# Steps listed from a block's landing, and a third column group turned by TensorE

## The chip, the cores and the metric

The kernel runs on one core of one Trainium2 chip. The metric is device time in microseconds (us) of one execution of the whole kernel; lower is better.

## What is computed

One layer of a streaming encoder on 512 frames of width 2048, in float32. One input projection feeds three token mixers of four heads each (forgetting, chunked and stick-breaking attention), a SiLU gate for each mixer and three merge gates for each channel. Then each mixer's output is projected up, weighted by its merge gate, the three are added, and one output projection is added to the input. The change lies in these last lines of the reference:

```python
    gates = jax.nn.sigmoid(proj[..., QKVG_COLS + N_HEADS:] + b_gate).reshape(b, s, N_BRANCH, D_MODEL)
    ...
    ys = ys * jax.nn.silu(br[:, :, :, 3])
    up = jnp.einsum('bsnw,nwd->bsnd', ys, w_up)
    merged = jnp.sum(gates * up, axis=2)
    return x + jnp.einsum('bsd,de->bse', merged, w_out)
```

## The kernel before

**Numbers.** A float32 product is made of three products of rounded parts: an operand is split into a high part (an ACT copy that rounds) and a low part (a DVE subtraction). For weights these are the tiles `wh` (L409) and `wl` (L419), for the other operand a `Parts` tile of both; `split` (L255 to L264) makes the latter. All main matmuls are L277. The input and output projections are done by Strassen's scheme with seven products, so they need differences of quarters of their operands too.

**Stages.** First the input projection with the attention of the heads beside it. Then the up projection, on which this case turns: its result `merged` is 512 frames by 2048 channels, in four *column groups* g of 512 channels. For each group and each of the three mixers (`UPS`, L1554, gives the order) there are two units of 24 matmuls (`up_units`, L1310). A unit treats its four row blocks of 128 frames one after another, six matmuls each. When a row block's sum stands in an accumulator (there are six, `accs`), `taken` (L1317) multiplies it by the gate, which ACT has put through a sigmoid (`gates_of`, L1297, line L1305) after a read from DRAM (L293): L1321, and for the second and third mixer adds it up: L1328. The order of `UPS` is groups 0 and 2 mixed, then group 1, then group 3. So group 1 is the third one done.

**Turning a group.** The output projection needs `merged` with channels on the partitions, so each group of 512 by 512 must be transposed. There are two ways. For groups in `DRAMS` (L1555: 0, 2 and 1), `folded` (L1350) lets DVE transpose 32x32 squares (L1354) and stores the four row blocks to DRAM (L301), and `turned_m` (L1361) reads each of the group's four channel blocks back with `back` (L307, four reads of 64 KB, L312), so that the squares land in their places. For the rest (group 3), `spun_m` (L1378) lets TensorE transpose (L1385) into a PSUM tile of which there are two (`atts`), four 128x128 transposes for each channel block, and ACT copies it out (L1392).

**Steps on a merged block.** `arrived` (L1370) numbers the blocks k = 4g + i and starts the steps that make the operands of the output projection's Strassen scheme. Blocks 0 to 7 (groups 0 and 1) get `merged_a` (L1398): one DVE subtraction (L1401) and a split (L258 on ACT, L262 on DVE) give `m1`. Blocks 8 to 15 (groups 2 and 3) get `merged_b` (L1406): they wait for `m1` of block k - 8, then make three differences (L268) and split them into `m23`, `m4` and `m2`. The first four units of the output projection use `m1` of blocks 0 to 3, the next four that of blocks 4 to 7 (`out_task`, L1461).

**What sets the order.** Each engine executes its own list of instructions in order, and the lists are written by a planner (`Flow`, L65) in the kernel's own program. A task is a generator that yields an engine and a cost for each step. The planner keeps a clock for each engine, takes the step that can start first and breaks ties by the due time, which is the time at which the task was ready plus its slack (L126). So a task's ready time and slack decide where a step stands in its engine's list. Nothing is decided again on the chip: there a step whose data isn't there yet holds all that stands behind it in the list. Transfers have a model of their landing (`landing`, L283, with `LAND` 3.5 and for `back` `PIECES` 4.0, L1560), in plan time. `spawn(gen, slack, ready)` starts a task; `flow.fin` is the planned end of the step that was just listed, and `flow.ready` the ready time of the task that is being advanced, which includes an event that it has passed. In `turned_m`, the last event before `arrived` is the landing plus `MEXTRA` (L1367). An event whose time is known doesn't stop a task, so `arrived` runs as soon as the last read is listed, and `flow.fin` is then the planned end of that read's issue (0.54 us for a read).

**Slots.** The tiles of 128x512 float32 (`t2s`, `NT` = 20 of them) serve gates, sums, merged blocks, differences and more. A task waits in the plan until one is free, and one with a slack over 1 leaves three (`KEPT`) free. `folded` gives the four tiles of a group back at the planned landing of their stores, `spun_m` gives all four back when the last of the group's channel blocks has been transposed, and takes a tile for each block at the copy.

**Other lists.** All reads and stores named here stand in SP's list with the loads of weights; POOL issues accumulating loads (L320) alone.

Of the kernel before, what the change touches and what calls it, by code (L numbers as in the profile page):

```python
# [25 lines left out]
UK = 8  # L26
# [38 lines left out]
class Flow:  # L65
# [16 lines left out]
    def give(self, slots, n=1):  # L82
        slots.free += [self.fin] * n

    def spawn(self, gen, slack, ready=None):
        task = Task(gen, slack, self.now if ready is None else ready)
        self.tasks.append(task)
        self.advance(task)
# [82 lines left out]
def dve_us(n, x=1):  # L171
    return x * (0.1 + 0.00105 * n)
# [3 lines left out]
def hybrid_kernel(  # L176
# [30 lines left out]
    flow = Flow()  # L207
    spawn, set_, give = flow.spawn, flow.set, flow.give
# [3 lines left out]
    def t2(s, dt=F32):  # L212
        return tp.tile([P, S], dt, tag="t2", name=nm(s))
# [13 lines left out]
    def blk(i):  # L227
        return slice(i * P, (i + 1) * P)
# [3 lines left out]
    def two(ap):  # L232

        return ap.rearrange("p (h s) -> p h s", h=2)
# [20 lines left out]
    def split(hi, lo, src, n, ev=None, due=(), hi_ev=None):  # L255

        yield (ACT, act_us(n), *due)
        nc.scalar.activation(hi, src, AF.Copy)  # L258
        if hi_ev is not None:
            set_(hi_ev)  # L260
        yield (DVE, dve_us(n), *due)
        nc.vector.tensor_sub(lo, src, f(hi))  # L262
        if ev is not None:
            set_(ev)  # L264

    def minus(to, a, b):

        nc.vector.scalar_tensor_tensor(to, a, -1.0, b, op0=ALU.mult, op1=ALU.subtract)  # L268
# [38 lines left out]
    def back(to, src):  # L307

        n = src.shape[0] * 4
        for b in range(4):  # L310
            yield issue(0.54)
            nc.sync.dma_start(to[32 * b:32 * (b + 1), :].rearrange("p (n c) -> p n c", c=32),  # L312
                              src.rearrange("t (a r) c -> (t a) r c", r=32)[:, :, 32 * b:32 * (b + 1)]
                              .rearrange("n r c -> r n c"))
            ev = Event(landing(flow.fin, n * 4, 128) + PIECES)
        return ev
# [60 lines left out]
    def at(u, g, slack=5.0):  # L377
        side.setdefault(u, []).append((g, slack))
# [971 lines left out]
    def folded(g, tb):  # L1350
        yield merged_ev[NB - 1, g, tb]
        m = merged[g, tb]
        yield DVE, dve_us(S) + 0.07
        nc.vector.transpose(m, m)  # L1354
        if g not in md:
            md[g] = dp.tile([QB, P, S], F32, name=nm("md"))
        md_ev[g, tb].t = (yield from store(md[g][tb], m, 256, t2s)).t + LATER
# [3 lines left out]
    def turned_m(g, i):  # L1361
        for tb in range(QB):
            yield md_ev[g, tb]
        yield t2s, 1
        m = t2("m")
        ev = yield from back(m, md[g][:, :, blk(i)])
        yield Event(ev.t + MEXTRA)  # L1367
        arrived(g, i, m)

    def arrived(g, i, m):  # L1370
        k = 4 * g + i
        if k < UK:
            kept_m[k] = m
            spawn(merged_a(k, m), 4.0, flow.fin)
        else:
            spawn(merged_b(k - UK, m), 3.0, flow.fin)

    def spun_m(g, i):  # L1378
        for tb in range(QB):
            yield merged_ev[NB - 1, g, tb]  # L1380
        yield atts, 1
        yield PE, 0.11 * QB
        ps = att()
        for tb in range(QB):
            nc.tensor.transpose(ps[:, blk(tb)], merged[g, tb][:, blk(i)], identf)  # L1385
        turns[g] = turns.get(g, 0) + 1
        if turns[g] == QB:
            give(t2s, QB)
        yield t2s, 1
        yield ACT, act_us(S)  # L1390
        m = t2("m")
        nc.scalar.activation(m, ps, AF.Copy)  # L1392
        give(atts)
        arrived(g, i, m)
# [3 lines left out]
    def merged_a(k, a):  # L1398

        yield DVE, dve_us(HS)  # L1400
        nc.vector.tensor_sub(a[:, RH], a[:, LH], a[:, RH])  # L1401
        yield xps, 1
        m1[k] = Parts("m1", [m1_ev[k]] * 2)
        yield from split(m1[k].hi, m1[k].lo, two(a), S, m1_ev[k])

    def merged_b(k, b):  # L1406
        a = kept_m[k]
        yield m1_ev[k]
        yield t2s, 1
        t = t2("mt")  # L1410
        if k % 2 == 0:
            yield t2s, 1
            mus[k // 2] = t2("mu")
        u = mus[k // 2][:, RH if k % 2 else LH]
        q = DVE, dve_us(HS)
        yield q
        minus(t[:, LH], b[:, RH], a[:, RH])
        yield q
        minus(t[:, RH], t[:, LH], a[:, LH])
        give(t2s)  # L1420
        yield q
        minus(u, t[:, LH], b[:, LH])
        yield xps, 1
        ev = Event()
        m23[k] = Parts("m23", [ev, ev])
        yield from split(m23[k].hi, m23[k].lo, two(t), S, ev)
        give(t2s)
        if k % 2 == 0:
            yield xps, 1
            m4[k // 2] = Parts("m4")  # L1430
            set_(m4_ev[k // 2])
        yield xps, 1
        ev = Event()
        m2[k] = Parts("m2", [ev, ev])
        yield from split(m2[k].hi, m2[k].lo, two(b), S, ev)
        give(t2s)
        yield m4_ev[k // 2]
        h, lo, ev = m4[k // 2].half(k % 2)
        yield from split(h, lo, u, HS, ev)
        if k % 2:  # L1440
            give(t2s)

    for g, b in UPS:
# [5 lines left out]
        for i in range(QB):  # L1449
            if g in DRAMS:  # L1450
                at(len(units) - 1, lambda g=g, i=i: folded(g, i))
# [100 lines left out]
NR = 8  # L1552

UPS = [(0, 0), (0, 1), (2, 0), (2, 1), (0, 2), (2, 2)] + [(g, b) for g in (1, 3) for b in range(3)]  # L1554
DRAMS = (0, 2, 1)  # L1555
MLATE, MSKIP = 2.5, 1

EARLY = 0.5
# [4 lines left out]
HSLACK = 12.0  # L1563
ENDSLACK, ENDOFF = 3.0, 3
EARLYG = 1
MEXTRA = 8.0

_OUT = (QB, NQ, P, S)

# [45 lines left out]
```

## Time and profile before

| | us |
|---|---|
| median of 3 runs | 1297.6 |
| lowest and highest run | 1290.79, 1299.38 |
| the profiled execution, its own time | 1294.25 |
| span of the profiled execution | 1292.5 |
| TensorE busy | 1274.2 (99%) |
| VectorE (DVE) busy | 999.5 (77%) |
| ScalarE (ACT) busy | 752.2 (58%) |
| DVE's subtractions L1401 waiting for reads of merged blocks | 16.3, in 2 waits |

All times of the trace count from the start of the span. PE is TensorE's matmul, PEld its weight load, SPq the list of transfers that SP issues. The granted clock is the share of full speed that TensorE had; its mean over the span is 0.996. The up projection lies between about 982 and 1126 us, the output projection behind it. The rows that the prediction rests on stand in it.

### The profile page before, as it was taken

The numbers are of one execution on the slowest core, as the hardware profiler recorded it, in microseconds if no ns is written. First come the engines' busy times: TensorE is split into PE (matmuls) and PEld (weight loads), VectorE is DVE, ScalarE is ACT, GpSimd is POOL, SyncE is SP. The second block draws the span as 40 slices with busy tenths as digits, with TensorE's granted clock in tenths as the row PEclk, the third lists the DMA queues.
The fourth block names the chain that finished last, engine by engine and source line by source line (L and its number), as shares of the span: only waits on it lengthen the run. The fifth ranks groups of instructions, "written<-read, shape, count | busy, mean of one in ns | idle before, by whom it ended". The sixth has DMA issues, their size and how long they took to land. (4 is left out here: it accounts for less than half of the span.)

```text
span 1292.5 us, 17358 instructions
## 1 busy us (share of the span) xinstructions
PE 1274.2 (99%) x5700; PEld 1050.2 (81%) x5700; DVE 999.5 (77%) x1402; ACT 752.2 (58%) x1239; POOL 91.7 (7%) x115
## 2 busy tenths in 40 slices
PE   9999999999999999999999999999999998989998
PEld 7788888888888888888888788887887786868887
DVE  6948896978969677686876878868788686898665
ACT  7836565645756567565575665755656532564442
POOL 0001010110101101011010110101100000010100
PEclk9999999999999999999999999999999999989999
DMA  9685899987889878897889978889889979946963
GB/s 356 207 206 123 216 235 215 265 200 209 222 201 281 191 218 228 199 272 196 222 223 208 271 183 220 230 192 287 189 217 342 286 228 211 265 94 224 238 169 129
DMA packets 269690, 286.51 MB, mean 222 GB/s; under 512 B 178320, under 2 KB 189072, under 8 KB 269600
## 3 DMA queue, kind: packets, MB, share of 16 engines
q1 hardware_dynamic: 252176, 226.42, 59.0%
q0 software_dynamic: 14976, 54.53, 22.6%
q10 hardware_dynamic: 2448, 4.46, 0.9%
q8 instruction: 45, 0.74, 0.2%
q14 instruction: 45, 0.37, 0.1%
HBM read 241.78 MB, written 43.56 MB: 221 GB/s over the span
## 5 line engine op out<-in xcount | busy, mean ns | idle before, releaser
L419 DVE TENSOR_TENSOR wl<-raw,wh 128x1024 fp32r<-128x1024 f32 (+1 forms) x405 | 492.5, 1217 | 215.5 <-PE acc L277 138.7
L409 ACT ACTIVATE wh<-raw 128x1024 fp32r<-128x1024 f32 (+1 forms) x404 | 426.0, 1056 | 359.8 <-PE acc L277 327.9
L277 PE MATMUL acc<-wh,x 128*128 128x512 f32 x1664 | 424.0, 390 | 0.1
L277 PEld LDWEIGHTS acc<-wh,x 128*128 128x128 f32 x1664 | 312.0, 188 | 68.4 <-issue 3.4
L277 PE MATMUL acc<-wh,t 128*128 128x512 f32 x1056 | 275.4, 390 | 2.4 <-ACT wh L409 2.4
L277 PEld LDWEIGHTS acc<-wh,t 128*128 128x128 f32 x1056 | 197.3, 188 | 43.2 <-ACT wh L409 3.3
L277 PE MATMUL acc<-wl,x 128*128 128x512 f32 x832 | 232.2, 389 | 0.1
L277 PEld LDWEIGHTS acc<-wl,x 128*128 128x128 f32 x832 | 155.8, 188 | 32.5 <-DVE wl L419 0.5
L277 PE MATMUL acc<-wl,t 128*128 128x512 f32 x528 | 154.6, 391 | 0.2
L320 POOL DMA_DIRECT2D raw<-in_w_col x88 | 76.1, 865 | 846.4 <-DMA raw<-in_w_col 136.7
L630 DVE TENSOR_TENSOR raw<-raw,raw 128x1024 f32<-128x1024 f32 x104 | 126.7, 1218 | 0.1
L277 PEld LDWEIGHTS acc<-wl,t 128*128 128x128 f32 x528 | 98.2, 188 | 21.5 <-DVE wl L419 2.0
L277 PE MATMUL acc<-wh,m 128*128 128x512 f32 x448 | 114.4, 389 | 0.0
L277 PE MATMUL acc<-wh,y 128*128 128x512 f32 x384 | 104.2, 393 | 0.0
L277 PEld LDWEIGHTS acc<-wh,m 128*128 128x128 f32 x448 | 84.0, 188 | 17.5
L277 PEld LDWEIGHTS acc<-wh,y 128*128 128x128 f32 x384 | 72.6, 189 | 15.1
L277 PE MATMUL acc<-wl,m 128*128 128x512 f32 x224 | 64.7, 395 | 5.7 <-DVE wl L419 5.7
L277 PE MATMUL acc<-wl,y 128*128 128x512 f32 x192 | 60.4, 394 | 4.2 <-DVE wl L419 4.2
L714 ACT ACTIVATE u<-acc 128x512 f32<-128x512 f32 x52 | 31.1, 599 | 41.4 <-PE acc L277 41.3
L277 PEld LDWEIGHTS acc<-wl,m 128*128 128x128 f32 x224 | 42.3, 190 | 15.1 <-DVE wl L419 6.5
L277 PEld LDWEIGHTS acc<-wl,y 128*128 128x128 f32 x192 | 36.4, 191 | 12.7 <-DVE wl L419 5.3
L1321 DVE TENSOR_TENSOR sg<-acc,sg 128x512 f32<-128x512 f32 x48 | 32.6, 685 | 7.2 <-ACT sg L1305 3.6
(155 smaller groups left out, 951.3 us busy)
## 6 DMA issues: line engine op xcount, KB each, us to landing
raw<-in_w_col SPq DMA_DIRECT2D x191, 512.0 KB, 5.0
raw<-in_w_col POOLq DMA_DIRECT2D x88, 512.0 KB, 8.2
raw<-in_w_out SPq DMA_DIRECT2D x32, 512.0 KB, 4.8
raw<-in_w_up SPq DMA_DIRECT2D x24, 512.0 KB, 4.9
sg<-gl SPq DMA_DIRECT2D x48, 256.0 KB, 5.2
gl<-u SPq DMA_DIRECT2D x44, 256.0 KB, 4.8
raw<-in_w_out POOLq DMA_DIRECT2D x16, 512.0 KB, 6.8
qkl<-qd SPq DMA_DIRECT2D x96, 64.0 KB, 4.0
```

What stands on the lines that cost most here:

```text
L277: nc.tensor.matmul(ps, w, x, start=start, stop=stop, skip_group_check=more)
L320: nc.gpsimd.dma_start(to, src, accum_op=ALU.add)
L409: nc.scalar.activation(u.hi, u.raw, AF.Copy)
L419: nc.vector.tensor_sub(u.lo, u.raw, f(u.hi))
L630: nc.vector.tensor_add(to.raw, to.raw, self.raw)
L714: nc.scalar.activation(t, w, AF.Copy)
L1321: nc.vector.tensor_mul(t, ps[tb], t)
```

## The change

Two things. In `arrived`, the steps on a merged block get the later of `flow.ready` and `flow.fin` as their ready time, in place of `flow.fin`; the slack of `merged_a` goes from 4.0 to 1.0 (that of `merged_b` stays 3.0), and `MEXTRA` from 8.0 to 4.0. And group 1 leaves `DRAMS`, so that it takes the way of `spun_m`.

```diff
@@ -1371,9 +1371,9 @@
         k = 4 * g + i
         if k < UK:
             kept_m[k] = m
-            spawn(merged_a(k, m), 4.0, flow.fin)
+            spawn(merged_a(k, m), MAS, max(flow.ready, flow.fin))
         else:
-            spawn(merged_b(k - UK, m), 3.0, flow.fin)
+            spawn(merged_b(k - UK, m), MBS, max(flow.ready, flow.fin))
...
-DRAMS = (0, 2, 1)
+DRAMS = (0, 2)
...
-MEXTRA = 8.0
+MEXTRA = 4.0
+MAS = 1.0
+MBS = 3.0
```

## The prediction

> **What bounds the kernel now.** I read the first block of the page, then the busy time in slices of 10 us, then the waits from 1000 us on, then the order of time on each engine around the two places that stood out.
>
> ```profile
> span 1292.5 us, 17358 instructions
> PE 1274.2 (99%) x5700; PEld 1050.2 (81%) x5700; DVE 999.5 (77%) x1402; ACT 752.2 (58%) x1239; POOL 91.7 (7%) x115
> ```
>
> TensorE is busy for 99% of the span, so work elsewhere counts only where TensorE stands still or runs slowly, and a gain is bounded by how much of that there is. The lists are written from front to back and the diff first acts at the reads of the first merged group, so only the time from about 1060 us on is in question. Its slices (columns: slice, its length, busy us of PE, PEld, DVE, ACT, POOL with counts, granted clock, DMA share, GB/s):
>
> ```profile
> 1070.00:1080.00 10.00, 7.55 (x34) 5.92 (x32) 2.17 (x5) 1.86 (x4) 0.00 (x0) 1.00 0.94 200
> 1080.00:1090.00 10.00, 8.28 (x28) 6.33 (x29) 9.96 (x15) 6.00 (x9) 0.86 (x1) 0.83 0.78 151
> ...
> 1130.00:1140.00 10.00, 4.29 (x16) 3.26 (x16) 7.70 (x13) 4.63 (x7) 0.00 (x0) 0.67 0.41 61
> ...
> 1160.00:1170.00 10.00, 10.00 (x46) 8.28 (x45) 9.68 (x14) 6.81 (x12) 0.00 (x0) 1.00 0.44 78
> ```
>
> An undisturbed slice starts some 46 matmuls. Three have 34, 28 and 16, two of them at a granted clock of 0.83 and 0.67: the loss is idle time and, after it, slow time. Who is waited for (us in total, times, longest), from 1000 us on:
>
> ```profile
> PE acc L277 <- DVE wl L419: 9.9, 3, 5.7
> DVE m L1401 <- DMA m<-md: 16.3, 2, 10.0
> ```
>
> TensorE waits for the low part of a weight block (L419, DVE); DVE, in front of it, waits for a read of a merged block (L1401, the first step of `merged_a`). The order of time shows it, first DVE, then PE, for both places (start, length, in brackets the idle time before it):
>
> ```profile
> 1066.41 1.22 DVE L419 TENSOR_TENSOR wl<-raw,wh 128x1024 fp32r<-128x1024 f32 x1
> 1077.68 1.43 DVE L1401 TENSOR_TENSOR m<-m 128x256 f32<-128x256 f32 x3 [10.05 <-DMA m<-md]
> ...
> 1079.62 1.22 DVE L419 TENSOR_TENSOR wl<-raw,wh 128x1024 fp32r<-128x1024 f32 x1
> ...
> 1132.27 0.43 DVE L1401 TENSOR_TENSOR m<-m 128x256 f32<-128x256 f32 x1 [6.25 <-DMA m<-md]
> ...
> 1135.54 1.22 DVE L419 TENSOR_TENSOR wl<-raw,wh 128x1024 fp32r<-128x1024 f32 x1
> ```
>
> ```profile
> 1076.48 1.07 PE L277 MATMUL acc<-wh,y 128*128 128x512 f32 x4
> 1080.89 0.73 PE L277 MATMUL acc<-wl,y 128*128 128x512 f32 x2 [3.34 <-DVE wl L419]
> ...
> 1126.41 1.98 PE L277 MATMUL acc<-wh,m 128*128 128x512 f32 x8
> ...
> 1136.82 2.08 PE L277 MATMUL acc<-wl,m 128*128 128x512 f32 x4 [5.71 <-DVE wl L419]
> ...
> 1142.14 1.04 PE L1385 MATMUL att<-identf,sg 128*128 128x128 f32 x8
> 1142.93 1.19 PE L277 MATMUL acc<-wl,m 128*128 128x512 f32 x4
> ...
> 1149.42 1.07 PE L277 MATMUL acc<-wh,m 128*128 128x512 f32 x4
> ```
>
> The reason is in the code. `arrived` spawns the step with `flow.fin`, the planned end of the read's last issue, so the step stands in DVE's list as if the data were there at issue. The four blocks of a group are read in four pieces each, and SP's list has the last four pieces of the first group only at 1073.01 and the last six of the third at 1127.43. The pieces land a median 4.5 us after issue, and DVE stands at the step until then. Rows of SP's list, and the last line of the view of tile `m`:
>
> ```profile
> 1073.01 2.20 SPq L312 DMA_DIRECT2D m<-md  x4
> ...
> 1106.53 5.21 SPq L293 DMA_DIRECT2D sg<-gl  x7
> ...
> 1113.56 13.30 SPq L312 DMA_DIRECT2D m<-md  x10
> ...
> 1127.43 3.71 SPq L312 DMA_DIRECT2D m<-md  x6
> ```
>
> ```profile
> DMA to landing us min/median/max: 2.9/4.5/10.0
> ```
>
> **What the two stalls cost.** The pitch of undisturbed matmuls comes from 1153 to 1285 us, by form: 132 us / (389 + 193) = 0.2268 us.
>
> ```profile
> L277 PE MATMUL acc<-wh,m 128*128 128x512 f32 x389 | 99.4, 389 | 0.0
> L277 PE MATMUL acc<-wl,m 128*128 128x512 f32 x193 | 55.1, 390 | 0.0
> ```
>
> First place: four matmuls start at 1076.48, so the next is due at 1077.39; the third stage ends with the first product of the output projection at 1126.41. Between them lie 32 pairs on wl and 31 fours on wh (8 units with 8 wl each), 188 matmuls, 42.6 us at the pitch. They took 49.0: **6.4 us** lost. Second place: from 1126.41 to 1149.42 lie 5 units of 12, 60 matmuls, 13.6 us, and 16 turnings. Eight turnings at full clock go from 1142.14 to 1142.93, 0.79 us; 16 are 1.6. The stretch took 23.0, so **7.8 us** are lost. Together 14.2 us, which is all that this change can win: behind 1150 the slices are full.
>
> **The change, part by part.**
>
> *Steps from the landing.* The step of the first group moves from the planned issue to the planned landing plus `MEXTRA`: by the constants in the code at least 1.0 + 0.42 + 3.5 + 4.0 + 4.0 = 12.9 us later in the plan. On the chip it needed 10.05 us, which contains SP's own lag. So the stall goes, with 2.9 us to spare, and a remainder of up to some 5 us would still be free, since 10.05 us of idle DVE became only 3.34 us of idle PE (a unit's weights are ready about one unit ahead). Value -6.4; bounds 0 (back in full) and -6.4. Who needs the moved steps? The first wh,m product, at 1126.41, some 40 us after the steps; 13 us are covered. `MAS` 1.0 in place of 4.0 only puts the moved steps ahead of others then due. Their DVE work is not new, but it goes into a busy stretch:
>
> ```profile
> 1077.30:1126.35 49.05, 44.88 (x190) 36.43 (x189) 46.96 (x77) 25.95 (x42) 3.45 (x4) 0.97 0.94 236
> L1401 DVE TENSOR_TENSOR m<-m x8: 417/425/427, 1077.7 to 1135.2; 128x256 f32<-128x256 f32 x8
> L262 DVE TENSOR_TENSOR m<-m,m x16: 681/686/690, 1079.0 to 1163.8; 128x512 fp32r<-128x512 f32 x16
> L1354 DVE STREAM_TRANSPOSE sg<-sg x12: 669/702/705, 1042.7 to 1101.6; 128x512 f32<-128x512 f32 x12
> L1392 ACT ACTIVATE m<-att x4: 594/598/602, 1139.8 to 1143.3; 128x512 f32<-128x512 f32 x4
> ```
>
> DVE had 46.96 us of work in that stretch, the first group's steps among them. Four transposes go (2.8 us) and the third group's four subtractions and low parts come forward into it (4 x 1.11 = 4.4): 48.6 us. There is room from 1067.6 (end of the last wl before the stall) to 1126.35 - 6.4 + 1.6 = 1121.5, 53.9 us. DVE is 90% full, not the bound. Cost 0.
>
> *Third group turned by TensorE.* Gone are 4 transposes on DVE, 4 stores and 16 reads on SP (the x10 and x6 rows), with their 2 MB of traffic. The second stall hangs on the last of these reads, so it goes as a whole: -7.8 (bounds: 0 and -7.8; 0 only if another wait falls on the same spot). New are 16 turnings on TensorE, which is the bound, so all of it counts: **+1.6**, by the row of 0.79 for eight. New are four copies of 0.60 us on ACT, which was busy 25.95 of 49.05: hidden; uncovered they would cost 2.4. The SP list loses 20 issues and nothing is added to it; POOL's list is not passed.
>
> The Trainium skill speaks against this part: "TensorE: Matmul & The Clock Gate", Part 4: PE-mode transpose, gives about 275 ns for one 128x128 turning in a kernel's context, and says the clock gate does not count it as activity. By that the 16 would be an estimated 4.4 us, and the total 1284.9 in place of 1282.1. The rows agree with the length of one, but eight in 0.79 us overlap, and with 16 of them so close to full matmuls I keep the pitch.
>
> *A new wait.* The turnings stand in TensorE's list behind the last addition of the group (L1328); behind them on PE are all later matmuls. Now the same wait of the fourth group, which is already turned so, is hidden behind the second stall; so there are two places. In the plan the turning follows the last matmul of its group by 0.3 + 2 x 0.64 + 0.12 + 0.25 = 1.95 us. On the chip:
>
> ```profile
> 1065.35 1.06 ACT L409 ACTIVATE wh<-raw 128x1024 fp32r<-128x1024 f32 x1 [3.34 <-PE acc L277]
> 1065.81 0.69 DVE L1321 TENSOR_TENSOR sg<-acc,sg 128x512 f32<-128x512 f32 x1 [0.67 <-PE acc L277]
> 1056.18 0.70 DVE L1328 TENSOR_TENSOR sg<-sg,sg 128x512 f32<-128x512 f32 x1
> ```
>
> The unit ends at 1065.35, the multiplication begins 0.46 later, and multiplication and addition take 0.69 and 0.70: 1.85 us, just in time. With one weight step (1.22) in front, 1.1 us late. Bounds 0 and 2.2 for the two; I take 0.5.
>
> *Slots.* The third group's blocks take their four t2 tiles when turned, some 15 us before the reads did. That is a rival, below.
>
> **The sum**, against the profiled execution's own 1294.25 us (span 1292.5 and 1.75 around it): 1294.25 - 6.4 - 7.8 + 1.6 + 0.5 = 1282.1. That execution lies 3.35 below the median of the three runs and 3.46 above the lowest; the mean of all four is 1295.5, 1.2 above it. Whether the spread comes from the two stalls, which depend on landings, or from elsewhere is not shown, so I put the forecast 1.2 higher: **1283.3 us**. Its own range is 1279 to 1288. A measurement of this kernel can tell about 1% from no change; 1% below the median is 1284.6, so the forecast is close to that line.
>
> **Rivals.**
>
> *A wait of slots takes part of it back* (chance 0.15). There are 20 t2 tiles and steps with a slack over 1 leave three free. Around the third group's turning hold: first group 4, second group 4, third group's sums 4, fourth group's gates up to 4, and a difference and its `mu` 2: 18 for 17. The turned blocks come ahead of the fourth group's gate reads (the x7 row at 1106.53). TensorE has six accumulators and a set of sums takes four, so the first accumulator of a set is wanted again five row blocks after its sum is done. A row block is 6 matmuls, 1.36 us: 6.8 us less the 0.69 of the multiplication leaves 6.1 us in which a late gate costs nothing. If the gates come 12 us later than the sums, TensorE stops for 6: 1283.3 + 6 = 1289. For it: the count. Against: the four sums come free at once when all are turned, not at their stores' landing, and the read queue has 2 MB less.
>
> *The same wait in full: slower* (0.10). If the gate reads wait until the last of the second group's blocks is done, they come some 20 us late; TensorE stops for 20 - 6.1 = 13.9, and pays slow time behind the gap too (the first loss had 6.4 - 3.5 = 2.9 behind its first gap): 1283.3 + 16.8 = 1300.1. It decides from about 18 us of delay on; from 30 us on it passes 1310. Against it: the second group's steps free tiles one after another, not all at the end.
>
> *The first stall stays* (0.07). If SP lags its plan by some 8 us more than now, the landing comes after the planned step again; the second stall is gone anyway, and the time is 1283.3 + 6.4 = 1289.7. Against: the SP list gets shorter and its waits on DVE were partly made by the stall itself.
>
> **Chances and range.** Forecast 0.68, rivals 0.15, 0.10, 0.07. Of the forecast's 0.68 about three quarters lie below 1284.6: faster by over 1% 0.50. The rest of it (0.18), the slots in part, the first stall and some 0.04 of the slots in full lie within 1%: 0.44. Slower by over 1%, above 1310, keeps the 0.06 of the slots in full with the longest delays. The range goes from 1278.5 (the lowest run, 1290.79, less 12.2) to 1292 (slots in part with an upper bound of 2.2 for the new wait): about 0.83 of the chance.
>
> **What would show it.** Right: no idle time before L1401 of more than 1 us; 12 transposes become 8 on DVE and 32 turnings stand on L1385; 32 reads m<-md; the granted clock is 1.00 in every slice from 1060 to 1280; PE idle behind L1385 under 1 us. Wrong: a PE wait on L1385 of several us, a wait of L1321 on the gate's sigmoid with PE idle behind it, or a DVE row on m<-md of over 5 us.

## The result, and the profile after

| | before | after |
|---|---|---|
| median of 20 runs, us | 1292.89 | 1285.74 |
| lowest and highest, us | 1289.14, 1302.02 | 1281.18, 1296.5 |
| the profiled execution's own time and span, us | 1294.25, 1292.5 | 1284.99, 1283.3 |

The ratio is 0.9947, 95% interval 0.9932 to 0.9962: 0.53% faster. The medians differ by 7.2 us, six tenths of the 12.2 us of the forecast's sum. The time lies in the range. With 17 more runs the median of before fell by 4.7 us, so part of the nearness of 1285.74 to 1283.3 is luck; the difference is the thing to judge by.

The spans differ by 9.2 us, but 3.4 of these lie ahead of the up projection, where both kernels have the same lists. (In the kernel before it begins at 986.2 us, not at the 982 given above.) The view of tile `y` has the first and the last start of the up projection's products on `wh` (before, then after):

```profile
L277 PE MATMUL acc<-wh,y x384: 387/389/628, 986.2 to 1125.7; 128*128 128x512 f32 x192
```

```profile
L277 PE MATMUL acc<-wh,y x384: 387/389/632, 982.8 to 1124.1; 128*128 128x512 f32 x192
```

From its first product to the first of the output projection the up projection takes 140.2 us before and 142.0 after; the output projection, from there to its last product, 161.8 and 154.4. So the second stall's 7.8 us are won (7.4), and in the up projection 6.4 should have been won and 1.6 paid, 135.4, and none of it is there.

The slices of after (columns as in the prediction):

```profile
1070.00:1080.00 10.00, 10.00 (x46) 8.29 (x45) 6.92 (x10) 3.80 (x5) 0.86 (x1) 1.00 1.10 249
1080.00:1090.00 10.00, 10.00 (x46) 8.28 (x45) 9.89 (x18) 3.78 (x6) 0.86 (x1) 1.00 0.98 169
...
1100.00:1110.00 10.00, 8.48 (x41) 6.50 (x40) 10.00 (x21) 7.59 (x15) 1.72 (x2) 1.00 0.72 192
1110.00:1120.00 10.00, 7.78 (x27) 5.97 (x26) 10.00 (x19) 6.74 (x12) 0.00 (x0) 0.83 0.93 283
1120.00:1130.00 10.00, 10.00 (x45) 8.26 (x44) 9.27 (x13) 4.86 (x8) 0.00 (x0) 1.00 0.01 2
```

The place of the first stall is full now, and a new hole stands 30 us behind it, with slow time in it as the old one had. What makes it is read from the order of time, PE first:

```profile
1090.58 1.03 PE L1385 MATMUL att<-identf,sg 128*128 128x128 f32 x8
1091.37 0.71 PE L277 MATMUL acc<-wl,y 128*128 128x512 f32 x2
...
1101.65 0.66 PE L1385 MATMUL att<-identf,sg 128*128 128x128 f32 x4 [0.49 <-ACT m L1392]
1102.06 0.71 PE L277 MATMUL acc<-wl,y 128*128 128x512 f32 x2
...
1104.72 0.66 PE L1385 MATMUL att<-identf,sg 128*128 128x128 f32 x4 [1.02 <-ACT m L1392]
1105.13 0.71 PE L277 MATMUL acc<-wl,y 128*128 128x512 f32 x2
...
1114.88 1.39 PE L277 MATMUL acc<-wh,y 128*128 128x512 f32 x4 [2.22 <-DVE sg L1321]
...
1124.81 1.98 PE L277 MATMUL acc<-wh,m 128*128 128x512 f32 x8
```

From 1091.37 to 1124.81 stand 116 matmuls, 26.3 us at the pitch, and eight turnings, 0.8. They took 33.4: 6.3 us lost, in two waits of turnings for ACT's copies, a wait for an accumulator, and slow time behind it. TensorE waits for a gate's multiplication on DVE and for copies on ACT. Before that, both had stood still for a gate:

```profile
1097.28 0.69 DVE L1321 TENSOR_TENSOR sg<-acc,sg 128x512 f32<-128x512 f32 x1 [3.80 <-ACT sg L1305]
```

```profile
1096.61 1.31 ACT L1305 ACTIVATE sg<-sg 128x512 f32<-128x512 f32 x2 [6.07 <-DMA sg<-gl]
```

And the gate is read late, because of what stands ahead of it in SP's list:

```profile
1074.36 6.88 SPq L312 DMA_DIRECT2D m<-md  x11
1081.33 0.80 SPq L293 DMA_DIRECT2D raw<-in_w_out  x1
1082.17 5.22 SPq L312 DMA_DIRECT2D m<-md  x5
1087.49 1.86 SPq L293 DMA_DIRECT2D raw<-in_w_out  x1
1089.39 0.91 SPq L293 DMA_DIRECT2D sg<-gl  x2
...
1102.32 1.57 SPq L293 DMA_DIRECT2D sg<-gl  x2
```

Two gates of the fourth group are issued at 1089.39 behind the second group's reads, and land 7 us later. ACT stands at their sigmoid for 6.07 us with everything behind it. DVE can't make up the 3.80 us that it stands in turn: it is busy for 10.00 of 10.00 us in both slices from 1100 to 1120. Before, ACT's longest wait for a gate between 1040 and 1200 us was 2.4 us.

### The profile page after: what moved, and what is told of

The parts are those of the page before. It is cut to its first block, busy times and chain, and to the rows that moved or that the text cites. A ratio compares the mean times of both kernels' runs of the same rounds, so it can differ in the third digit from the quotient of the medians.

```text
span 1283.3 us, 17347 instructions
## 1 busy us (share of the span) xinstructions
PE 1272.8 (99%) x5716; PEld 1050.5 (82%) x5716; DVE 996.6 (78%) x1398; ACT 754.6 (59%) x1243; POOL 91.5 (7%) x115
## 4 chain that ended last, share of the span: by engine, by line
PE 91%; DMA 5%; DVE 3%; SPq 1%; issue 1%; ACT 0%; DVEq 0%; ACTq 0%; POOLq 0%
PE acc L277 87%; DMA sg<-gl 1%; DMA raw<-in_w_col 1%; DMA al<-pd 1%; DVE wl L419 1%; PE att L273 1%; PE att L274 1%; PE att L272 1%; PE att L1113 1%; PE att L1112 1%; PE att L1111 1%; DMA raw<-in_w_up 1%; DVE m L262 1%; DMA gl<-v 0%; SPq L293 0%
## 5 line engine op out<-in xcount | busy, mean ns | idle before, releaser
L277 PE MATMUL acc<-wl,t 128*128 128x512 f32 x528 | 154.4, 391 | 0.1
L1321 DVE TENSOR_TENSOR sg<-acc,sg 128x512 f32<-128x512 f32 x48 | 32.7, 687 | 13.1 <-ACT sg L1305 8.3
L1305 ACT ACTIVATE sg<-sg 128x512 f32<-128x512 f32 x48 | 28.1, 621 | 24.7 <-DMA sg<-gl 24.6
```

What stands on the lines that cost most here:

```text
L277: nc.tensor.matmul(ps, w, x, start=start, stop=stop, skip_group_check=more)
L1305: nc.scalar.activation(t, t, AF.Sigmoid)
L1321: nc.vector.tensor_mul(t, ps[tb], t)
```

## The experiments

Two theories went in. **S** (slots), the rival of the prediction: the gates are late since t2 tiles come free late. **Q** (queue): they are late since SP's list runs late behind the reads in pieces, and ACT, standing at the sigmoid, holds DVE and TensorE. Times of the up projection are those of the one profiled execution of each. Ratios are to the kernel before, with 95% intervals.

The time of the up projection has to be read with care. In all thirteen traces TensorE, ACT and DVE have the same steps in the same order up to the 193rd of its 576 products (the first of the ninth unit, at 1033.0 us before and 1029.8 after). Yet the way from the first product to that one takes between 45.7 and 50.6 us, so that much comes from the single execution and not from the experiment. The table splits each time there. The last column is what is lost behind the 193rd product: the time from it to the output projection, less 384 products at the pitch of 0.2268 us (87.1) and the turnings in between at 0.099 each (none in before and e1, 48 in e4, else 16).

| us | to the 193rd product | from there on | lost there |
|---|---|---|---|
| before | 46.8 | 93.4 | 6.4 |
| after | 47.0 | 95.0 | 6.3 |
| e1 | 46.4 | 93.3 | 6.2 |
| e2 | 49.4 | 94.6 | 5.9 |
| e3 | 50.6 | 96.9 | 8.2 |
| e4 | 48.0 | 92.6 | 0.7 |
| e5 | 45.7 | 90.5 | 1.8 |
| e6 | 50.1 | 95.7 | 7.0 |
| e7 | 47.4 | 88.9 | 0.2 |
| e8 | 47.2 | 90.8 | 2.1 |
| e9 | 47.2 | 91.0 | 2.3 |
| e10 | 46.4 | 88.9 | 0.3 |
| e11 | 48.1 | 89.5 | 0.8 |

**The halves.** e1 is the change with `DRAMS = (0, 2, 1)`; e2 keeps the turning and lists the steps as before, from their read's issue:

```diff
-            spawn(merged_a(k, m), MAS, max(flow.ready, flow.fin))
+            spawn(merged_a(k, m), MAS, flow.fin)
...
-MAS = 1.0
+MAS = 4.0
```

(and so for `merged_b`).

> The first half of the change alone: steps listed from the landing, group 1 still turned through DRAM. Theory S (slots: the fourth group's gate reads come late because t2 tiles come free late) and theory Q (queue: SP's list runs late behind the reads in 128-byte pieces, and the gate reads stand behind them) both expect the first DVE wait (10.05 us) gone. Both expect the gate reads late here too: the first 6.4 us won are given back in part (3 to 6 us) before the output projection. At the second place the blocks still land some 9 us after the output projection begins, so TensorE waits for m1 of blocks 4 to 7 itself, 3 to 6 us in place of 7.8. Sum: 1286 to 1292 us. If the landing listing were harmless by itself and only the turned blocks' tiles did the harm, the up projection would take 134 us (140.2 before, less 6.4) from its first product to its last.

Measured: 1290.16 us, 0.9973 (0.9957 to 0.999). The up projection takes 139.7 and the output projection 160.0. The expectation holds: of the 6.4 won next to nothing is left, TensorE waiting 3.5 us for an accumulator with slow time behind it. At the second place it waits 2.4 us for ACT's copies (L258, the high parts of `m1`) in place of 5.7 for a weight.

> The second half alone: group 1 turned by TensorE, steps listed from the read's issue as before (slack 4.0). Both theories expect the first DVE wait of about 10 us and its 6.4 us to stay, the second (7.8 us) to go, 16 turnings to cost 1.6: -6.2, 1287 us, with the up projection at 140 to 143 us and the output projection at 154.4 as after. If the turned blocks' tiles alone made the gates late, TensorE would lose some further 4 to 6 us at an accumulator here too: 1291 to 1293.

Measured: 1286.71 us, 0.9943 (0.9922 to 0.9963). The DVE wait at L1401 is there (9.3 us), the output projection takes 153.9, the up projection 144.0, the upper edge of what was expected; 2.4 of that lie ahead of the 193rd product (49.4 against 47.0). So the second half alone is as fast as both: in the changed kernel, listing from the landing adds nothing that shows. That what it wins is lost at the gates is what the next runs have to show.

**Slots.** e3 lets one tile be kept in place of three from the second half of the third group on:

```diff
+    def keep():
+        t2s.kept = 1
+        return
+        yield
+    at(len(units) - 7, lambda: keep())
```

> The changed kernel, but from the last unit but two of the up projection's third group on, steps with a slack over 1 leave one t2 tile free in place of three; so the fourth group's gate reads are listed earlier by up to 15 us. Theory S expects the PE wait for an accumulator and the slow time behind it (about 4 us) and the two waits of the turnings for their copies (1.5 us) mostly gone: the up projection at 137 to 138 us in place of 142.0, 1281 us. Theory Q expects SP's list to be as late as after (its reads of merged blocks stand where they stood), the first gate waits on ACT to stay at about 6 us, and a gain of under 2 us: 1284 to 1286.

Measured: 1289.48 us, 0.998 (0.9961 to 0.9999): slower than after. Its profiled execution is a long one (span 1295.6), with the up projection at 147.5; of that, 3.6 us more than in after lie ahead of the 193rd product, and 1.9 behind it. There ACT waits for gates nine times, 18.1 us in total, and a turning waits 4.9 us for ACT's copy:

```profile
1109.76 1.11 PE L1385 MATMUL att<-identf,sg 128*128 128x128 f32 x4 [4.91 <-ACT m L1392]
```

The gain that S expected does not come, although the edit does what S asks for: counted from the 193rd product, the two reads of the row at 1089.39 are issued at 55.4 and 56.0 us in place of 59.6 and 60.0. But their sigmoids stand earlier in ACT's list too, and ACT waits there 4.8 us all the same, and 3.3 us at a later gate. So earlier tiles do bring some gates earlier, and that is not enough.

**Queue, without the reads.** e4 has `DRAMS = ()`.

> All four column groups turned by TensorE, no reads in 128-byte pieces at all and 32 turnings more than after. Their pitch of 0.099 us makes +3.2 us on TensorE. Theory Q expects the gate reads on time and the 6.3 us lost in the up projection gone: -6.3 + 3.2, 1283 us, ACT waiting for gates under 2 us at one time. Theory S expects the blocks to hold tiles even earlier, so gates at least as late and the loss to stay: 1289 us.

Measured: 1285.24 us, 0.9938 (0.9914 to 0.9961). ACT waits for a gate once, 1.7 us, and no wait on TensorE is listed between 1040 and 1200 us. The up projection takes 140.5, with 4.8 us of turnings in it against 1.6 after. The gates are on time; the turnings eat more than half of what that wins. The up projection is 1.6 us longer than Q expected (142.0 - 6.3 + 3.2 = 138.9); 1.0 of these lie ahead of the 193rd product, and 0.7 are lost behind it.

**Queue, by another list.** e5 changes who issues the fourth group's gate reads, and the planner's lists of PE, ACT and DVE are step for step those of after:

```diff
+        if g == 3:
+            yield POOL, 0.9
+            nc.gpsimd.dma_start(t, gl[n, g, tb])
+            yield Event(landing(flow.fin, 256, 2048))
+        else:
+            yield (yield from fetch(t, gl[n, g, tb], 256))
```

> The changed kernel with the twelve gate reads of the fourth group issued by POOL in place of SP, so that they no longer stand behind the reads of merged blocks; the steps on the other engines keep their places. Theory Q (SP's list runs some 8 us behind the plan at these reads, and ACT stands at the gate's sigmoid with all behind it) expects ACT's waits for gates of over 3 us gone, no PE wait for an accumulator, the up projection at 135.5 to 137.5 us in place of 142.0: 1280 to 1281.5 us. Theory S (t2 tiles come free late) expects the gates no earlier than the planner lists them, the accumulator wait to stay: 1285 or more.

Measured: 1280.89 us, 0.9921 (0.9894 to 0.9948). The interval overlaps that of after, so it is the stage that has to tell. The up projection takes 136.2, 5.8 less than after; 4.5 of these lie behind the 193rd product. POOL issues the two gates 11.5 us ahead of SP's 1089.39 (9.9 us ahead, counted from the 193rd product), and their sigmoids start without a wait; PE's largest wait is 0.91 us (POOL, ACT, PE):

```profile
1077.91 1.41 POOL L1304 DMA_DIRECT2D sg<-gl  x2
```

```profile
1088.82 1.14 ACT L1310 ACTIVATE sg<-sg 128x512 f32<-128x512 f32 x2
...
1098.56 0.63 ACT L1310 ACTIVATE sg<-sg 128x512 f32<-128x512 f32 x1 [3.00 <-DMA sg<-gl]
```

```profile
1110.40 1.20 PE L277 MATMUL acc<-wh,y 128*128 128x512 f32 x4 [0.91 <-DVE sg L1326]
```

One thing expected was not so: ACT still waits 4.4 us at one gate. That gate is of the third group and is read by SP here too; after has a wait of 3.4 us at the same sigmoid. At the fourth group's gates the longest wait is the 3.00 us above. With the slots, and with the order of the steps on TensorE, ACT and DVE, as they were in after, 4.5 of the 6.3 us lost are gone: they came from the place of the gates in SP's list.

**Earlier listing, and a later sigmoid.** e6 has `MEXTRA = -4.0` and `MAS = 6.0`. e7 is e6 with

```diff
-        yield (yield from fetch(t, gl[n, g, tb], 256))
+        ev = yield from fetch(t, gl[n, g, tb], 256)
+        yield Event(ev.t + (6.0 if g == 3 else 0.0))
```

> The changed kernel with the extra 4.0 behind the landing turned into -4.0 and the slack of the first step 6.0: steps on a merged block are listed 8 us earlier than after, some 5 us before the planned landing was to be trusted, so tiles come free earlier. All theories expect a DVE wait at the first step of up to 6 us that costs TensorE nothing. Theory S expects the gates earlier by as much and the accumulator wait gone: up projection 136 to 137 us, 1280. Theory Q expects SP to be as late as it was and ACT to wait for gates 4 to 6 us at one time; of the 6.3 us lost it expects at most 3 back: 1283 to 1286.

Measured: 1283.91 us, 0.9943 (0.9923 to 0.9964), as after. The up projection takes 145.8 (a long execution, span 1289.1, of which 3.1 us more than in after lie ahead of the 193rd product); ACT waits 7.77 us for a gate and a turning 4.39 us for ACT. S's 1280 is missed, and the two gates are issued no earlier: 59.7 us behind the 193rd product, 59.6 in after.

> As e6, and the sigmoid of the fourth group's gates listed 6 us later than the planned landing of the gate, which is what SP lags. Theory Q expects ACT's waits for gates under 2 us each and with them DVE's and PE's behind them gone: up projection 135.5 to 137 us, 1280 us, some 3 us below e6. Theory S expects the same time as e6, within 1.5 us, since the tiles come free as there.

Measured: 1279.38 us, 0.9915 (0.9886 to 0.9944); up projection 136.3, no wait on PE between 1040 and 1200 us. ACT's longest wait for a gate is still 3.8 us, not under 2, but at a gate of the third group; at those of the fourth it has no wait over 0.2 us. The sigmoid that ACT stands at in e6 runs no earlier here: counted from the 193rd product it starts at 67.2 us in e6, at 68.2 in e7 and at 68.6 in e10, the same kernel as e7. What has moved is its place in ACT's list. In e6 it stands ahead of all four copies of the turned blocks, in e7 and e10 behind three of them (e6, then e10):

```profile
1102.65 0.63 ACT L1305 ACTIVATE sg<-sg 128x512 f32<-128x512 f32 x1 [7.77 <-DMA sg<-gl]
...
1106.00 1.05 ACT L1392 ACTIVATE m<-att 128x512 f32<-128x512 f32 x2
```

```profile
1094.27 0.58 ACT L1393 ACTIVATE m<-att 128x512 f32<-128x512 f32 x1
...
1096.53 0.62 ACT L1306 ACTIVATE sg<-sg 128x512 f32<-128x512 f32 x1
```

So lateness alone is not the price: the list that stands at it is.

> e5 and e6 together: gates by POOL and steps listed 8 us earlier. If both late gates and late tiles count, this is the fastest: up projection 135.4 us (134 less 0.2, and 1.6 for the turnings), 1279.5 us. If the queue is all, the same as e5 within 1 us.

Measured: 1284.07 us, 0.9942 (0.9919 to 0.9965); up projection 137.9. Missed: it should have been the fastest. A turning waits 1.7 us for ACT and ACT 4.9 us for a gate: with tiles free earlier the sigmoids stand earlier again. Behind the 193rd product, though, it takes 90.8 us and e5 90.5, the same within 1 us, as for the queue alone. Of the 4.0 us between the spans of the two profiled executions, 2.5 lie ahead of the up projection and 1.5 between its first and its 193rd product, where their lists are the same. Why all four executions of e8 were longer than those of e5 stays open.

> The changed kernel with nothing else altered but the sigmoid of the fourth group's gates listed 3 us later on ACT. If it is ACT's place in line that turns late gates into lost time (theory Q), its longest wait for a gate falls from 6.1 to some 3 us and DVE's behind it (3.8) to under 2; the gates stay late for their sums, so a wait for an accumulator may stay. Up projection 138 to 140.5 us in place of 142.0, 1283 us. If lateness of the gates alone counts, nothing changes: 142 us, 1286.

e9 is the changed kernel with 3.0 in place of 6.0 in the lines above, and nothing else. Measured: 1284.67 us, 0.9933 (0.991 to 0.9956), not to be told from after by the whole time; up projection 138.2, 3.8 less than after. ACT's wait at the two gates falls from 6.07 to 3.04 us, DVE's behind it to 1.0, TensorE's for an accumulator to 1.4. These are the sizes that Q expected, but this run does not show Q's reason. Up to these two sigmoids and one step beyond, ACT's list is that of after, so they have not moved. The first of the two gates landed earlier instead, 4.3 us after issue in place of 7.2:

```profile
1096.21 0.90 SPq L293 DMA_DIRECT2D sg<-gl  x2
```

```profile
1100.48 0.63 ACT L1306 ACTIVATE sg<-sg 128x512 f32<-128x512 f32 x1 [3.04 <-DMA sg<-gl]
```

How much of the 4.0 us won behind the 193rd product is due to that, and how much to the later place of the group's other sigmoids, stays open.

> The kernel of e7 once more, for a narrower interval: 0.990 to 0.993 of before, 1280 us, clearly below the changed kernel's 0.9947.

Measured: 1279.59 us, 0.9901 (0.9884 to 0.9918); up projection 135.3, the 135.4 that the two stalls and the turnings leave, with 0.3 us lost behind the 193rd product. Its turnings have no waits:

```profile
1086.83 1.03 PE L1386 MATMUL att<-identf,sg 128*128 128x128 f32 x8
1093.16 0.60 PE L1386 MATMUL att<-identf,sg 128*128 128x128 f32 x4
1094.07 0.60 PE L1386 MATMUL att<-identf,sg 128*128 128x128 f32 x4
```

> As e10, with the steps on merged blocks listed 2 us later than there (-2.0 and slack 3.0). If e7's gain is the mechanism and not a lucky order, this neighbour has it too: up projection 135.5 to 137.5 us, no PE wait of over 1 us, 0.990 to 0.993, 1280 us.

e11 has `MEXTRA = -2.0` and `MAS = 3.0`. Measured: 1280.99 us, 0.9919 (0.9895 to 0.9943); up projection 137.6, 0.1 above the edge, with 1.7 us more than e10 ahead of the 193rd product and 0.5 behind it; longest PE wait 0.4 us. The neighbour has the gain too. The version of e10 beats both kernels and e6: its interval lies clear of after's 0.9932 to 0.9962 and of e6's.

## Why the prediction was right, and where it was not

- **The stalls.** Right. DVE has no wait at L1401 in the profile after. The second stall's 7.8 us show as 7.4 in the output projection, the first one's 6.4 only once the gates are out of the way (e10: 0.3 us lost behind the 193rd product, against 6.4 before). The prediction's signs of being right held in part: 8 transposes on DVE, 32 turnings and 32 reads are there, but the granted clock falls to 0.83 in one slice, and one turning waits 1.02 us. One of its signs of being wrong is there too, a wait of L1321 on the gate's sigmoid (3.80 us) with TensorE idle behind it.
- **The turnings.** Right. The rows above give 1091.37 - 1090.58 = 0.79, and twice 0.41: 1.6 us for sixteen. The estimate of 4.4 us from the length that the Trainium skill gives for one ("TensorE: Matmul & The Clock Gate", Part 4: PE-mode transpose, about 275 ns) is not borne out. The length is the same here, a median of 272 ns, but in a row they overlap and cost 0.1 us each.
- **The new wait.** This step failed: "Bounds 0 and 2.2 for the two; I take 0.5." It looked at the turnings and at DVE, and at who stands behind them on PE. The turnings never waited for the last addition. They waited for ACT's copies, and an accumulator for a gate: 6.3 us in all. The prediction had seen that the first group's landing contains SP's own lag, and used it for the step that it costed. It did not ask what else stands behind the same reads on SP: the fourth group's gates. Counted from the 193rd product, the sigmoid of the first of the two gates starts at 67.7 us before and at 66.8 after: the gate is no later than it was. While DVE's wait lasted, TensorE was late too and the gate was in time; with the wait gone, it was the next to be late. A second term failed with it, DVE's "Cost 0": 48.6 us of work in 53.9 leave room only while DVE never stands. It stood 3.80 us at the gate and had no gap afterwards to make up for it.
- **The rival of slots** had the place and the size (gates late, an accumulator, 6 us, 1289), but not the cause. e3 and e6 give tiles earlier and win nothing, though in e3 two gates are read some 4 us earlier; e5 leaves the tiles as they are and wins 4.5 us behind the 193rd product.
- **The forecast's level.** 1.2 us were added for the spread of the runs; over 20 runs the median of before lies 1.4 below the profiled execution instead. The difference fell 5.0 us short (7.2 for 12.2), and the level gave 2.6 of them back, by luck. The prediction left open whether the spread comes from the two stalls. The 193rd product starts anywhere between 1027.9 and 1040.8 us in the thirteen traces, so a good part of it arises ahead of them.

Open: why SP's reads in pieces take what they take at some places (below), what e9 owes to the earlier landing, why e8's executions are longer than e5's, and what makes the time ahead of the 193rd product differ.

## What to carry to other kernels

Where lists are written ahead, compare each queue's issue times on the chip with the places that the plan gave them, and correct all that stands behind a late queue, not only the step whose stall is seen: a stall removed on one engine shows the next step that trusted the same queue. A step that waits for a transfer should stand in its list where the transfer really lands; a late transfer costs little (e7 against e6), a list that stands still for it costs all behind it. A spare queue for urgent reads (e5) does nearly the same as an honest place in the list. And an experiment on one stage is best judged from the last point up to which all lists are the same, not from the stage's start.

## What the runs showed of the hardware

The 32 reads of 64 KB in pieces of 128 bytes have a median issue of 0.487 us on SP, and single ones take up to 1.99:

```profile
L312 SPq DMA_DIRECT2D m<-md x32: 423/487/1990, 1055.9 to 1085.8; - x32
```

Five of them took 5.22 us in the row above. No run here tells what holds them. The gates by POOL landed later after their issue than those by SP (median 8.6 us in e5 between 1070 and 1118, 5.8 after between 1085 and 1118), and were in time all the same.

Behind the stop of TensorE of 2.22 us in after came slow time: the granted clock is 0.66 from 1115 to 1120. Behind the stop of 1.43 us in e9 it stayed at 1.00 (the two rows below). In the thirteen traces, from 100 us on and up to the last products, there are 12 stops of 2.2 to 5.7 us. Behind each, slow time at a granted clock of 0.50 begins 2.0 to 4.6 us after the stop does, and lasts 3.4 or 6.8 us. Of four stops of 1.6 to 1.9 us one has it (1.64 in e2; 1.69 in e8, 1.74 in e4 and 1.89 in e11 do not), and of those of 0.8 to 1.5 us none. In between, the length of a stop alone does not decide; what does is not shown.

```profile
1115.00:1120.00 5.00, 5.00 (x15) 3.97 (x16) 5.00 (x10) 1.74 (x4) 0.00 (x0) 0.66 0.86 300
```

```profile
1117.00:1122.00 5.00, 3.58 (x15) 2.44 (x14) 4.97 (x10) 1.65 (x5) 0.00 (x0) 1.00 1.00 377
```
